# Two broadcasts in a two-layer backbone kernel: through DRAM with a broadcast DMA, in place of matmuls

## The chip, the cores and the metric

The kernel runs on one core of one Trainium2 chip. The metric is the time of one execution on the device in microseconds (us), as the median of several runs. The engines are TensorE (PE; PEld are its weight loads), VectorE (DVE), ScalarE (ACT), GpSimd (POOL) and SyncE (SP), which in this kernel only issues DMAs, one after another from one queue.

## The reference

Two layers, each: a normalisation modulated by c, three token mixers side by side, and one output projection. Cut to what matters here:

```python
def layer_fwd(x, xc, c, c_ctx, ...):                  # x: (1, 256, 1024) latent, xc: (1, 256, 1024) context
    shift, scale, gate = split(silu(c) @ w_mod + b_mod, 3)
    shift_c, scale_c, gate_c = split(silu(c_ctx) @ w_mod + b_mod, 3)
    h  = rms_norm(x, norm_g) * (1 + scale) + shift    # hc for xc in the same way
    p  = [h @ w for w in split_cols(w_in, IN_SIZES)]
    y_a = ssd_branch(...)      # bidirectional scan over chunks of 128 tokens, 16 heads, decays exp(cumsum)
    y_b = diff_branch(...)     # differential attention
    y_c = mlstm_branch(...)    # bidirectional matrix memory over chunks of 128 tokens, 4 heads,
                               # with a running maximum as stabiliser
    mixed = (g[0] * (y_a @ w_branch[0]) + g[1] * (y_b @ w_branch[1]) + g[2] * (y_c @ w_branch[2])) @ w_out
    x_new = x + gate[:, None] * mixed                 # xc_new = xc + gate_c * ...
```

All of it is in float32. The output is x after the second layer.

## The kernel before

The 256 context and 256 latent tokens are four chunks (NT = 4) of P = 128 tokens; group p = 0 is the context, p = 1 the latent tokens. Every float32 operand of a large product is split in a high and a low part (`whi`/`wlo` for weights, `hh`/`hl` for the normalised input, `yh`/`yl` for a branch output), and a product is three matmuls, hi*hi, hi*lo and lo*hi: lines L148 to L150 where tokens stand on the partitions of the result (`mm_tok`), L179 to L181 where channels do (`proj_ch`). Weights come as `raw` tiles of 512 KB (three buffers), ScalarE casts `whi` (L119) and DVE subtracts `wlo` (L82; the helper `tt` puts all its tensor_tensor operations on that line, `stt` on L79).

The order of the instructions on each engine is made by the framework's scheduler from priorities that the source sets with `band(0)`, `band(1)` and `band(2)`: 0 for weight loads, splits and evacuations, 1 for scans and attention, 2 for the projections' matmuls. All DMAs stand in SP's one queue in the order that results.

**The row stage**, once in each layer, makes the per-token numbers of the two scans. The gate rows lie on NR = 64 partitions (two directions of 32) with 512 tokens along the row. At each chunk's end three values for each row are put into `sv` [64, 3, 4] (L613 and lines before it): the end of the cumulated log decay, the running maximum that the chunk starts with, and the one it ends with. Meanwhile r1 and r2 are transposed to tokens on partitions (L626; `ca` and `cb` are the copies, L630). Tokens on partitions also need the twelve end values of each row on every partition: the tile `bcs` [128, 12, 64]. It is made on PE: `sx` is `sv` spread on a diagonal (a product with the identity), and a matmul with ones sums over its 64 partitions, in two halves of 384 columns (L637), each copied from PSUM to `bcs` (L638). From `bcs`, `ca` and `cb` come the columns `col` (SSD) and `mlc` (mLSTM), which scale the operands of the scans. In the same stretch of the program, DVE makes `ux` (SSD inputs after the convolution), which PE transposes (L710), and between these PE runs projections' matmuls.

**The output stage**, once in each layer: the gate `modc[l][:, 16:24, cc]` has channels on partitions (8 columns of 128 channels, cc = 1 for context), and the result has tokens on partitions. So `gbc[p]` [128, 1024] is to hold the gate along the row, the same on every partition. For each of its eight blocks of 128 channels one column of `modc`, repeated 128 times as the stationary operand, is multiplied with the identity (L1247), and ScalarE copies each half from PSUM with a factor 0.5 (L1249). The factor belongs to the merge's sigmoid. `evac_out` multiplies the accumulated output projection by `gbc[p]` (`otmp`) and adds it to the residual (`y`). In layer 0 both groups are worked on, in layer 1 only the latent one, so there are three gbc tiles. The last weight tiles of layer 0's output projection take the buffers `yh`/`yl` (L1297).

Of the kernel before, what the change touches and what calls it, by code (L numbers as in the profile page):

```python
# [14 lines left out]
ALU = mybir.AluOpType  # L15
# [3 lines left out]
D = 1024  # L19
P = 128  # L20
# [9 lines left out]
NR = 64  # L30
# [4 lines left out]
def hybrid_backbone_kernel(ctx: ExitStack, tc: tile.TileContext, A, out, dbg=None):  # L35
    nc = tc.nc
    V, S, G, T = nc.vector, nc.scalar, nc.gpsimd, nc.tensor
# [5 lines left out]
    @contextmanager  # L43
    def band(b):
        saved = tc.cur_priority
        tc.cur_priority = bands[b]
        yield
        bands[b] = tc.cur_priority
        tc.cur_priority = saved

    base = ctx.enter_context(tc.tile_pool(name="base", bufs=1))
    psum = ctx.enter_context(tc.tile_pool(name="psum", bufs=1, space=PSUM))

    def mk(pool, shape, tag, dt=F32, bufs=1):
        if dbg is not None:
            b = 1
            for n in shape[1:]:
                b *= n
            b *= 2 if dt == BF16 else 4
            key = (pool.name, tag)  # L60
            dbg["usage"][key] = max(dbg["usage"].get(key, 0), (b + 31) // 32 * 32 * bufs)
        return pool.tile(list(shape), dt, tag=tag, name=tag, bufs=bufs)

    def pacc():
        return mk(psum, [P, 512], "acc", bufs=ACC)
# [4 lines left out]
    def pm():  # L70
        return mk(psum, [P, 512], "pm", bufs=PM)
# [6 lines left out]
    def stt(o, a, s, b, op0, op1, eng=None):  # L78
        (eng or V).scalar_tensor_tensor(out=o, in0=a, scalar=s, in1=b, op0=op0, op1=op1)  # L79

    def tt(o, a, b, op, eng=None):
        (eng or V).tensor_tensor(out=o, in0=a, in1=b, op=op)  # L82
# [10 lines left out]
    def bc(ap, n):  # L93

        return ap.unsqueeze(len(ap.shape)).to_broadcast(list(ap.shape) + [n])


    ident = mk(base, [P, P], "ident")
# [3 lines left out]
    ones = mk(base, [NR, P], "ones")  # L102
# [6 lines left out]
    modc = [mk(base, [P, 24, 2], "modc", bufs=2) for _ in range(depth)]  # L109
# [340 lines left out]
    for l in range(depth):  # L450
# [84 lines left out]
        rp = tc.alloc_tile_pool(name=f"row{l}", bufs=1)  # L535
# [24 lines left out]
        with band(1):  # L560
# [39 lines left out]
            sv = mk(rp, [NR, 3, NT], "sv")  # L600
            V.memset(sv, 0.0)
            for i in range(NT):
                for d, order in ((0, FWD), (1, BWD)):
                    c = order[i]
# [24 lines left out]
            V.tensor_copy(ca, pa.rearrange("p (c r) -> p c r", r=P))  # L629
            V.tensor_copy(cb_, pb.rearrange("p (c r) -> p c r", r=P))  # L630

            sx = mk(rp, [NR, 12, NR], "sx")
            tt(sx, bc(sv.rearrange("p a c -> p (a c)"), NR), ident[0:NR, 0:NR].unsqueeze(1).to_broadcast([NR, 12, NR]), ALU.mult)
            bcs = mk(rp, [P, 12, NR], "bcs")
            for i in range(2):
                pt = pm()
                T.matmul(pt[:, 0:384], lhsT=ones, rhs=sx[:, 6 * i : 6 * i + 6, :].rearrange("p a r -> p (a r)"), start=True, stop=True)  # L637
                V.tensor_copy(bcs[:, 6 * i : 6 * i + 6, :], pt[:, 0:384].rearrange("p (a r) -> p a r", r=NR))  # L638
            acl, mpb, meb = bcs[:, 0:4, :], bcs[:, 4:8, :], bcs[:, 8:12, :]
            for d in range(2):  # L640
                r_ = slice(32 * d, 32 * d + 16)
# [9 lines left out]
            for d in range(2):  # L651
                r_ = slice(32 * d + 16, 32 * d + 20)
# [66 lines left out]
        chunk = lambda a, c: a[:, c * P : (c + 1) * P]  # L719
# [518 lines left out]
        xnew = Tokens(yx, "y", pq) if not last else xcur  # L1238
        with band(1):
            gbc = {}  # L1240
            for p in pq:
                gbc[p] = mk(ep, [P, D], "gbc", bufs=2)
                cc = 1 - p
                for hf in range(2):
                    pt = pm()
                    for k in range(4):
                        T.matmul(chunk(pt, k), lhsT=modc[l][:, 16 + 4 * hf + k, cc : cc + 1].to_broadcast([P, P]), rhs=ident, start=True, stop=True)  # L1247

                    S.mul(gbc[p][:, hf * 512 : (hf + 1) * 512], pt, 0.5)  # L1249
            if l == 0:  # L1250
                for p in pq:
                    for i in range(2):
                        for g in range(2):
                            src = (A["x"] if p else A["ctx"])[0][i * P : (i + 1) * P, g * 512 : (g + 1) * 512]
                            nc.sync.dma_start(xnew.tile(g, 2 * p + i), src)
# [11 lines left out]
        def evac_out(p, b, ps):  # L1267
            x_ = xnew(b, p)
            tmp = mk(ep, [P, 2, 256], "otmp", bufs=2)
            tt(tmp, ps, gbc[p][:, b * 256 : (b + 1) * 256].unsqueeze(1).to_broadcast([P, 2, 256]), ALU.mult)  # L1270
            tt(x_, x_, tmp, ALU.add)
            if last:
                for i in range(2):
                    nc.sync.dma_start(out[0][i * P : (i + 1) * P, b * 256 : (b + 1) * 256], x_[:, i, :])
# [3 lines left out]
        for b in range(2):  # L1278
            ps = {}
            with band(2):  # L1280
                for p in pq:
                    ps[p] = pacc()
            for k0, hi, lo in granules([wo(b)]):
                with band(2):
                    for p in pq:
                        mm_tok(ps[p], lhs, p * 256 - off, k0, hi, lo)
            for p in pq:
                with band(0):
                    evac_out(p, b, ps[p].rearrange("p (t n) -> p t n", t=2))
# [10 lines left out]
        for p in pq:  # L1300
            for b in (2, 3):
                cs = slice((b - 2) * 256, (b - 1) * 256)
                with band(2):
                    ps = pacc()
                    for g in range(2):
                        mm_tok(ps, lhs, p * 256 - off, 4 * g, wh[:, 4 * g : 4 * g + 4, cs], wl[:, 4 * g : 4 * g + 4, cs])
                with band(0):
                    evac_out(p, b, ps.rearrange("p (t n) -> p t n", t=2))
# [61 lines left out]
```

## Time and profile before

| | |
|---|---|
| median of 3 runs | 1710.55 us (1707.45 to 1711.42) |
| the profiled execution | 1711.2 us, of which the span of the trace is 1709.1 us |
| PE busy | 1677.3 us, 98% of the span |
| DVE busy | 1115.3 us, 65% |
| ACT busy | 762.7 us, 45% |
| POOL busy | 164.0 us, 10% |
| mean granted clock of PE | 0.992 of full speed |

The busy time is that of instructions which the profiler recorded. In rows of the trace, `out<-in` are the program's names of the tiles, a size is partitions x elements, `xN` stands for N instructions, and a bracket at the end of a row says how long the engine stood idle before it and what ended that. The granted clock (PEclk) is a share of the full 2.4 GHz.

### The profile page before, as it was taken

Reading aid. Unit: us, or ns where it says so; the run is one execution under the profiler, and the core shown is the slowest. Engines: PE = TensorE matmul, PEld = TensorE weight load, DVE = VectorE, ACT = ScalarE, POOL = GpSimd, SP = SyncE. Lnnn points to the kernel's source line nnn. Section 1 sums busy time; section 2 is a strip of 40 time slices with the busy share of each in tenths; the row PEclk is TensorE's granted clock in tenths of the full one; section 3 lists DMA queues with packets and bytes.
Section 4 is the critical chain, followed back from the end, with each engine's and each line's share of the span. In section 5 each row is a group of like instructions: output and inputs, shape, how many; then the busy total and the mean of one; then the engine's idle time right before and its main releaser. Section 6 shows DMA issues by size and latency. Waiting matters only on the chain.

```text
span 1709.1 us, 28774 instructions
## 1 busy us (share of the span) xinstructions
PE 1677.3 (98%) x11448; PEld 1489.2 (87%) x11448; DVE 1115.3 (65%) x2183; ACT 762.7 (45%) x1501; POOL 164.0 (10%) x192
## 2 busy tenths in 40 slices
PE   5999999999999999999999999999999999999998
PEld 2787889999899999977777789988999999999998
DVE  4698887667865666623334354898877867765565
ACT  3455644554544444422223233455555555444453
POOL 0102422101100000000010002012121100000100
PEclk8999999999999999999999999999999999999999
DMA  8522122222222222353544442322242324335654
GB/s 262 128 75 62 50 63 65 73 75 63 76 63 75 64 73 64 125 178 96 182 136 131 163 129 51 108 67 75 79 131 71 101 66 130 93 111 173 179 170 146
DMA packets 191906, 180.38 MB, mean 106 GB/s; under 512 B 20606, under 2 KB 177920, under 8 KB 191772
## 3 DMA queue, kind: packets, MB, share of 16 engines
q1 hardware_dynamic: 191772, 178.54, 35.6%
q8 instruction: 90, 1.47, 0.4%
q14 instruction: 44, 0.36, 0.1%
HBM read 177.47 MB, written 1.05 MB: 104 GB/s over the span
## 4 chain that ended last, share of the span: by engine, by line
PE 91%; DVE 4%; DMA 2%; issue 1%; ACT 1%; POOL 0%; SPq 0%; DVEq 0%; ACTq 0%; POOLq 0%
PE acc L149 12%; PE acc L148 12%; PE acc L150 12%; PE acc L179 12%; PE acc L181 12%; PE acc L180 12%; PE pe L917 2%; PE pm L935 2%; DMA wm<-in_w_mod_dram 1%; PE pm L743 1%; PE pm L1088 1%; PE pm L1067 1%; PE pe L228 1%; PE pe L1072 1%; PE pm L775 1%
## 5 line engine op out<-in xcount | busy, mean ns | idle before, releaser
L82 DVE TENSOR_TENSOR wlo<-raw,whi 128x1024 fp32r<-128x1024 f32 x274 | 348.8, 1274 | 308.4 <-ACT whi L119 306.9
L149 PE MATMUL acc<-wlo,hh 128*128 128x256 f32 x1728 | 504.9, 292 | 0.0
L150 PE MATMUL acc<-whi,hl 128*128 128x256 f32 x1728 | 503.1, 291 | 0.0
L148 PE MATMUL acc<-whi,hh 128*128 128x256 f32 x1728 | 501.5, 290 | 0.0
L119 ACT CAST whi<-raw 128x1024 fp32r<-128x1024 f32 x274 | 287.8, 1051 | 383.7 <-PE acc L180 255.0
L149 PEld LDWEIGHTS acc<-wlo,hh 128*128 128x128 f32 x1728 | 330.7, 191 | 12.6 <-issue 9.3
L150 PEld LDWEIGHTS acc<-whi,hl 128*128 128x128 f32 x1728 | 330.8, 191 | 10.4 <-issue 8.4
L148 PEld LDWEIGHTS acc<-whi,hh 128*128 128x128 f32 x1728 | 330.6, 191 | 10.0 <-issue 7.6
L179 PE MATMUL acc<-hh,whi 128*128 128x512 f32 (+1 forms) x712 | 256.3, 363 | 0.0
L180 PE MATMUL acc<-hl,whi 128*128 128x512 f32 (+1 forms) x712 | 254.9, 359 | 0.1
L181 PE MATMUL acc<-hh,wlo 128*128 128x512 f32 (+1 forms) x712 | 253.5, 357 | 0.0
L179 PEld LDWEIGHTS acc<-hh,whi 128*128 128x128 f32 x712 | 134.6, 190 | 27.0 <-issue 6.4
L180 PEld LDWEIGHTS acc<-hl,whi 128*128 128x128 f32 x712 | 135.1, 190 | 19.7 <-issue 3.0
L181 PEld LDWEIGHTS acc<-hh,wlo 128*128 128x128 f32 x712 | 135.1, 190 | 19.5 <-issue 1.9
L179 PE MATMUL acc<-yh,whi 128*128 128x512 f32 (+1 forms) x384 | 128.7, 338 | 0.0
L180 PE MATMUL acc<-yl,whi 128*128 128x512 f32 (+1 forms) x384 | 128.3, 336 | 0.0
L181 PE MATMUL acc<-yh,wlo 128*128 128x512 f32 (+1 forms) x384 | 128.2, 336 | 0.0
L921 ACT ACTIVATE E<-pe,nmax 128x512 f32<-128x512 f32 (+1 forms) x96 | 58.7, 617 | 46.9 <-DVE nmax L919 46.8
L181 PEld LDWEIGHTS acc<-yh,wlo 128*128 128x128 f32 x384 | 71.9, 188 | 8.2
L180 PEld LDWEIGHTS acc<-yl,whi 128*128 128x128 f32 x384 | 72.1, 188 | 8.0
L179 PEld LDWEIGHTS acc<-yh,whi 128*128 128x128 f32 x384 | 72.0, 188 | 7.3
L919 DVE TENSOR_REDUCE nmax<-pe 128x1 f32<-128x512 f32 (+1 forms) x96 | 53.8, 595 | 20.2 <-PE pe L917 19.9
(302 smaller groups left out, 2510.7 us busy)
## 6 DMA issues: line engine op xcount, KB each, us to landing
raw<-in_w_in_dram SPq DMA_DIRECT2D x192, 512.0 KB
raw<-in_w_branch_dram SPq DMA_DIRECT2D x48, 512.0 KB
wm<-in_w_mod_dram SPq DMA_DIRECT2D x45, 512.0 KB
raw<-in_w_in_dram SPq DMA_DIRECT2D x48, 256.0 KB
raw<-in_w_out_dram SPq DMA_DIRECT2D x16, 512.0 KB
raw<-in_w_mod_dram SPq DMA_DIRECT2D x3, 512.0 KB
xin<-in_ctx_dram SPq DMA_DIRECT2D x2, 512.0 KB
xin<-in_x_dram SPq DMA_DIRECT2D x2, 512.0 KB
```

The source lines that it names most:

```text
L82: (eng or V).tensor_tensor(out=o, in0=a, in1=b, op=op)
L119: S.copy(hi, raw)
L148: T.matmul(o, lhsT=xh[:, k, sl], rhs=hi[:, j, :], start=(k == 0 and i == 0), stop=False)
L149: T.matmul(o, lhsT=xh[:, k, sl], rhs=lo[:, j, :], start=False, stop=False)
L150: T.matmul(o, lhsT=xl[:, k, sl], rhs=hi[:, j, :], start=False, stop=(k == KT - 1 and i == 1))
L179: T.matmul(o, lhsT=hi[:, j, cs], rhs=xh[:, k, a:b], start=(k == 0 and first), stop=False)
L180: T.matmul(o, lhsT=hi[:, j, cs], rhs=xl[:, k, a:b], start=False, stop=False)
L181: T.matmul(o, lhsT=lo[:, j, cs], rhs=xh[:, k, a:b], start=False, stop=(k == KT - 1 and final))
L917: T.matmul(es[m][0], lhsT=x[own, qs], rhs=y[own, 0:N], start=(n == 0), stop=(n == 2))
L919: V.tensor_reduce(out=ng[:, m : m + 1], in_=es[m][0], axis=AX.X, op=ALU.max, negate=True)
L921: S.activation(e_, o, AF.Exp, bias=ng[:, m : m + 1], accum_out=rs[:, m : m + 1])
L935: T.matmul(po[:, qs], lhsT=chunk(aT, kt), rhs=vt[:, kt, h * P : (h + 1) * P], start=(kt == 0), stop=(kt == nk - 1))
```

## The change

The values go to DRAM and come back with a DMA that reads the same row for all 128 partitions. In the row stage two DMAs write `sv` (32 rows each, four-byte elements, 384 of them) to a DRAM tile `sv_d` [12, 64], and one DMA broadcasts its 768 values to `bcs` (128 x 3 KB, 393 KB). In the output stage one DMA for each token group writes the gate to `gate_d` (1024 four-byte elements), and one broadcasts it to `gbc` (128 x 4 KB, 512 KB). The factor 0.5 moves into `evac_out`, which takes a scalar_tensor_tensor for the tensor_tensor. `rows_d` is the DRAM pool. All these DMAs are issued by SP, at band 0.

```diff
--- before.py
+++ after.py
@@ -49,6 +49,7 @@
         tc.cur_priority = saved
 
     base = ctx.enter_context(tc.tile_pool(name="base", bufs=1))
+    rows_d = ctx.enter_context(tc.tile_pool(name="rows_d", bufs=1, space=bass.MemoryType.DRAM))
     psum = ctx.enter_context(tc.tile_pool(name="psum", bufs=1, space=PSUM))
 
     def mk(pool, shape, tag, dt=F32, bufs=1):
@@ -629,13 +630,12 @@
             V.tensor_copy(ca, pa.rearrange("p (c r) -> p c r", r=P))
             V.tensor_copy(cb_, pb.rearrange("p (c r) -> p c r", r=P))
 
-            sx = mk(rp, [NR, 12, NR], "sx")
-            tt(sx, bc(sv.rearrange("p a c -> p (a c)"), NR), ident[0:NR, 0:NR].unsqueeze(1).to_broadcast([NR, 12, NR]), ALU.mult)
+            sv_d = mk(rows_d, [12, NR], "sv_d", bufs=2)
             bcs = mk(rp, [P, 12, NR], "bcs")
-            for i in range(2):
-                pt = pm()
-                T.matmul(pt[:, 0:384], lhsT=ones, rhs=sx[:, 6 * i : 6 * i + 6, :].rearrange("p a r -> p (a r)"), start=True, stop=True)
-                V.tensor_copy(bcs[:, 6 * i : 6 * i + 6, :], pt[:, 0:384].rearrange("p (a r) -> p a r", r=NR))
+            with band(0):
+                for r_ in (slice(0, 32), slice(32, NR)):
+                    nc.sync.dma_start(sv_d.rearrange("a r -> r a")[r_, :], sv[r_].rearrange("p a c -> p (a c)"))
+                nc.sync.dma_start(bcs.rearrange("p a r -> p (a r)"), sv_d.rearrange("a r -> (a r)").partition_broadcast(P))
             acl, mpb, meb = bcs[:, 0:4, :], bcs[:, 4:8, :], bcs[:, 8:12, :]
             for d in range(2):
                 r_ = slice(32 * d, 32 * d + 16)
@@ -1238,15 +1238,13 @@
         xnew = Tokens(yx, "y", pq) if not last else xcur
         with band(1):
             gbc = {}
+            gate_d = mk(rows_d, [2, D], "gate_d", bufs=2)
             for p in pq:
                 gbc[p] = mk(ep, [P, D], "gbc", bufs=2)
                 cc = 1 - p
-                for hf in range(2):
-                    pt = pm()
-                    for k in range(4):
-                        T.matmul(chunk(pt, k), lhsT=modc[l][:, 16 + 4 * hf + k, cc : cc + 1].to_broadcast([P, P]), rhs=ident, start=True, stop=True)
-
-                    S.mul(gbc[p][:, hf * 512 : (hf + 1) * 512], pt, 0.5)
+                with band(0):
+                    nc.sync.dma_start(gate_d[cc].rearrange("(k p) -> p k", p=P), modc[l][:, 16:24, cc])
+                    nc.sync.dma_start(gbc[p], gate_d[cc].partition_broadcast(P))
             if l == 0:
                 for p in pq:
                     for i in range(2):
@@ -1267,7 +1265,8 @@
         def evac_out(p, b, ps):
             x_ = xnew(b, p)
             tmp = mk(ep, [P, 2, 256], "otmp", bufs=2)
-            tt(tmp, ps, gbc[p][:, b * 256 : (b + 1) * 256].unsqueeze(1).to_broadcast([P, 2, 256]), ALU.mult)
+
+            stt(tmp, ps, 0.5, gbc[p][:, b * 256 : (b + 1) * 256].unsqueeze(1).to_broadcast([P, 2, 256]), ALU.mult, ALU.mult)
             tt(x_, x_, tmp, ALU.add)
             if last:
                 for i in range(2):
```

What this does to the order of the instructions is shown at three places. On DVE in the row stage of layer 0, before, this is the stretch from the first readers of `bcs` to the third `ux` of that layer (which PE's third group of transposes at L710 reads):

```order
L82 TENSOR_TENSOR col<-bcs,ca 128x4x16
L646 COPY col<-bcs 128x4x16
L82 TENSOR_TENSOR col<-bcs,ca 128x4x16
L646 COPY col<-bcs 128x4x16
L826 TENSOR_REDUCE ssq<-sq 128x8
L82 TENSOR_TENSOR col<-col 128x128
L638 COPY bcs<-pm 128x384
L82 TENSOR_TENSOR mlc<-bcs,cb 128x4x4
L82 TENSOR_TENSOR mlc<-cb,bcs 128x4x4
L79 SCALAR_TENSOR_TENSOR ux<-th,cv_a 128x512
```

Now the stretch from the end of the rows' work (`r_z`) on; lines are shifted by one:

```order
L87 TENSOR_SCALAR r_z_566<-r_z 64x512
L83 TENSOR_TENSOR sm<-r_z_566,sm 64x512
L83 TENSOR_TENSOR wlo<-raw,whi 128x1024
L631 COPY cb<-pm 128x512
L83 TENSOR_TENSOR col<-bcs,ca 128x4x16
L646 COPY col<-bcs 128x4x16
L80 SCALAR_TENSOR_TENSOR ux<-th,cv_a 128x512
L83 TENSOR_TENSOR col<-bcs,ca 128x4x16
L646 COPY col<-bcs 128x4x16
L83 TENSOR_TENSOR mlc<-bcs 128x4x4
```

`sx` and the copies from `pm` are gone, and the first row that needs the broadcast stands right behind `cb`, with the third `ux` behind it. In layer 1 the third `ux` stands ahead of the first such row.

On SP at the same place, before, between the loads of small columns (`gcol`) and weights:

```order
L1167 DMA gcol<-in_ssd_a_log_dram 16x1
L1167 DMA gcol<-in_ml_i_bias_dram 4x1
L130 DMA raw<-in_w_in_dram 128x4x128 x2
L130 DMA raw<-in_w_in_dram 128x4x256 x17
L1167 DMA dbc<-in_ssd_d_dram 128x16
```

and now:

```order
L1167 DMA gcol<-in_ssd_a_log_dram 16x1
L1167 DMA gcol<-in_ml_i_bias_dram 4x1
L131 DMA raw<-in_w_in_dram 128x4x128 x2
L637 DMA sv_d<-sv 32x12x1 x2
L638 DMA bcs<-sv_d 128x768
L131 DMA raw<-in_w_in_dram 128x4x256 x17
L1167 DMA dbc<-in_ssd_d_dram 128x16
```

The two writes and the broadcast stand between the weight loads: the writes wait for `sv`, the broadcast for the writes, and the 17 weight loads behind them for their turn in the queue.

On SP at the end of layer 0, before:

```order
L130 DMA raw<-in_w_out_dram 128x4x256 x2
L1255 DMA y<-in_x_dram 128x512 x2
L130 DMA raw<-in_w_out_dram 128x4x256 x2
L1297 DMA raw<-in_w_out_dram 128x4x256 x3
L1255 DMA y<-in_x_dram 128x512 x2
L1297 DMA raw<-in_w_out_dram 128x4x256
```

and now:

```order
L131 DMA raw<-in_w_out_dram 128x4x256 x2
L1253 DMA y<-in_x_dram 128x512 x2
L131 DMA raw<-in_w_out_dram 128x4x256 x2
L1296 DMA raw<-in_w_out_dram 128x4x256
L1247 DMA gbc<-gate_d 128x1024 x2
L1246 DMA gate_d<-modc 128x8x1
L1296 DMA raw<-in_w_out_dram 128x4x256 x2
L1253 DMA y<-in_x_dram 128x512 x2
L1296 DMA raw<-in_w_out_dram 128x4x256
```

The two broadcasts of layer 0 and the write of layer 1's gate stand behind the first of the `yh` weight loads (L1297 before, L1296 now). The writes of layer 0's gate stand some thirty rows further up, and the broadcast of layer 1 twenty-odd rows further down. On PE the sixteen records at each gate and the L637 rows are gone, and the third group of `ux` transposes in layer 0 has 27 weight matmuls ahead of it since the r2 transposes; the wait ahead of the r2 transposes has the same rows before it.

## Rows read from the trace of the kernel before

**Rows 1.** The page: busy time by engine, and the chain that ended last.

```profile
PE 1677.3 (98%) x11448; PEld 1489.2 (87%) x11448; DVE 1115.3 (65%) x2183; ACT 762.7 (45%) x1501; POOL 164.0 (10%) x192
...
PE 91%; DVE 4%; DMA 2%; issue 1%; ACT 1%; POOL 0%; SPq 0%; DVEq 0%; ACTq 0%; POOLq 0%
```

**Rows 2.** Windows, in order: start:end, length, busy PE PEld DVE ACT POOL, PEclk, DMA, GB/s.

```profile
983.00:1026.00 43.00, 43.00 (x275) 37.31 (x275) 21.97 (x27) 15.81 (x20) 0.00 (x0) 1.00 0.45 127
...
1625.00:1667.00 42.00, 42.00 (x357) 42.00 (x356) 25.58 (x36) 22.36 (x36) 1.44 (x2) 1.00 0.59 172
...
1126.70:1133.70 7.00, 7.00 (x25) 4.97 (x23) 5.42 (x24) 1.35 (x4) 0.00 (x0) 0.51 0.51 150
```

**Rows 3.** Chain that ended last, gate's matmuls: start, us, what.

```profile
922.37 0.89 PE pm L1247 x8
...
1012.23 1.78 PE pm L1247 x16
```

**Rows 4.** The same chain in the two row stages.

```profile
113.36 0.84 PE pm L637 x2
...
115.10 0.12 PE acc L149
...
118.29 0.44 PE pm L710 x4
...
1127.48 1.57 PE pm L637 x2
...
1132.77 1.28 PE pm L637 x2
```

**Rows 5.** PE's timeline, the r2 transposes of both layers, with the wait before.

```profile
112.70 0.66 PE L626 MATMUL pm<-ident,r 128*128 128x128 f32 x4 [1.68 <-ACT r L619]
...
1125.51 0.66 PE L626 MATMUL pm<-ident,r 128*128 128x128 f32 x4 [2.02 <-ACT r L619]
```

**Rows 6.** DVE's timeline, row stage of layer 0.

```profile
111.23 0.32 DVE L613 COPY sv<-r_z 32x1 f32<-32x1 f32 x2
...
114.27 1.23 DVE L82 TENSOR_TENSOR wlo<-raw,whi 128x1024 fp32r<-128x1024 f32 x1 [0.26 <-ACT whi L119]
...
115.41 0.68 DVE L630 COPY cb<-pm 128x512 f32<-128x512 f32 x1
...
118.83 0.69 DVE L79 SCALAR_TENSOR_TENSOR ux<-th,cv_a 128x512 f32<-128x512 f32 x1
```

**Rows 7.** DVE's timeline, row stage of layer 1.

```profile
1124.05 0.31 DVE L613 COPY sv<-r_z 32x1 f32<-32x1 f32 x2
...
1131.02 0.23 DVE L82 TENSOR_TENSOR col<-bcs,ca 128x64 f32<-128x64 f32 x1
```

**Rows 8.** Timelines of SP and DVE: a broadcast load and its reader; the last store.

```profile
712.16 0.34 SPq L1167 DMA_DIRECT2D lamt<-in_diff_lambda_dram  x1
...
715.82 0.29 DVE L82 TENSOR_TENSOR lp<-lamt 128x128 f32<-128x128 f32 x1 [2.43 <-DMA lamt<-in_diff_lambda_dram]
...
1706.14 0.43 SPq L1274 DMA_DIRECT2D out_dram<-y  x1
```

**Rows 9.** Timelines of SP and ScalarE: the narrow columns of w_in (L548), and their cast.

```profile
1020.88 4.63 SPq L548 DMA_DIRECT2D raw<-in_w_in_dram  x6
...
1027.97 2.00 ACT L119 CAST whi<-raw 128x1024 fp32r<-128x1024 f32 x2 [6.38 <-DMA raw<-in_w_in_dram]
```

**Rows 10.** Waits of PE, 86 to 260 us: total us, times, longest.

```profile
PE pm L775 <- DVE M L82: 0.8, 1, 0.8
...
PE pm L743 <- DVE xw L82: 0.5, 1, 0.5
```

**Rows 11.** DVE's groups by line and shape: busy us, mean ns; then idle before.

```profile
L82 DVE TENSOR_TENSOR otmp<-acc,gbc 128x512 f32<-128x512 f32 x12 | 8.2, 683 | 12.8 <-PE acc L150 12.6
```

**Rows 12.** ScalarE's timeline; PE's instructions on yh (x, min/median/max ns, first to last).

```profile
1020.54 1.05 ACT L119 CAST yh<-raw 128x1024 fp32r<-128x1024 f32 x1 [2.20 <-DMA raw<-in_w_out_dram]
...
L148 PE MATMUL acc<-yh,yb x64: 278/281/375, 1032.6 to 1056.6; 128*128 128x256 f32 x64
```

## The prediction

> **What bounds the kernel now.** I read the page first: TensorE (PE) is busy for 1677.3 of 1709.1 us, and the chain that ended last is PE for 91% [rows 1]. So a matmul that is taken out gives its time back, as long as PE has other work ready there and none of what replaces it comes late. I then read the table of windows around each place that the change touches. In the stretches with the gate's matmuls PE has no idle time at all (43.00 of 43.00 us, and 42.00 of 42.00 us), while VectorE (DVE) is busy for 21.97 and 25.58 us of them [rows 2]. The stretch around the gates at 922 us looks the same. So in these stages PE alone sets the pace. The third row of the group is the row stage of layer 1: PE is busy for all of 7.00 us, at a granted clock of 0.51, which is the lower of its two levels (1.2 GHz against 2.4).
>
> The chain gives the price of each removed matmul, since it counts what a group adds to PE's time and not its pipelined length [rows 3, 4]. The timeline of PE shows why the row stage is not full of work: in both layers PE stands for 1.68 and 2.02 us until ScalarE has written r, ahead of the r2 transposes (L626) [rows 5]. The second of these waits is followed by the stretch at 0.51, the first by none. This wait lies ahead of everything that is changed, so I expect it to stay as it is.
>
> **What the change removes.**
> 1. The gate's matmuls (L1247): for each of three token groups eight, which the trace records as sixteen, half of them for each half of gbc. The chain has them as four groups of eight records with 0.89 us each (one stands for the four) and one of sixteen with 1.78 us [rows 3]. 4 x 0.89 + 1.78 = 5.34 us, all in stretches where PE has no gap. What stood behind them is weight products whose operands lay ready, so I count all 5.34 as gained.
> 2. The row stage's matmuls (L637): 0.84 us twice in layer 0 (one stands for both) and 1.57 + 1.28 = 2.85 us in layer 1, at the lower clock [rows 4]. At the full clock the latter are 2 x 0.84 = 1.68 us too. I take 1.68 for layer 1, because the lower clock is not theirs: a stretch at 0.51 that does its work in fewer cycles may end later in the work by as much. 2.85 is the other bound.
> 3. On DVE the building of sx, four copies bcs<-pm, and on ScalarE the six scalings by 0.5. All of it lies off the chain in stages where DVE and ScalarE have idle time. I count nothing for it. The factor 0.5 goes into the evacuation of the output: a SCALAR_TENSOR_TENSOR on 128x512 took 0.69 us [rows 6], the TENSOR_TENSOR that it replaces 683 ns [rows 11]. That is also nothing; if it cost a tenth more, the last evacuation alone would show at the end, by under 0.1 us.
>
> **What it adds.** Two hops through DRAM for each group, all issued by SyncE (SP).
>
> 4. The gates. The writes of layer 0 stand in SP's queue between weight loads of the branch projections, some 30 rows of SP ahead of their gbc, and the write and the gbc of layer 1 are as far apart. So the writes are hidden, and so is the gbc of layer 1, which goes out ahead of that layer's branch projections. At the end of layer 0 two gbc transfers of 512 KB each enter ahead of the w_out loads. In the stretch around it the DMA engines move 127 GB/s at a share of 0.45 [rows 2], so they could move about 127 / 0.45 = 282 GB/s, and 1.05 MB takes them about 3.7 us. The last of the loads behind them is cast at 1020.54 for 1.05 us, and PE reads the first of these weights at 1032.6 [rows 12]. That leaves 1032.6 - 1021.6 - 1.2 (the matching wlo, as in [rows 6]) = 9.8 us, more than 3.7. I count nothing. Without that cover it would be up to 3.7 us.
>
> 5. The end values in layer 0. The last copy to sv ends at 111.55 [rows 6]. SP issues two writes; an issue takes 0.34 to 0.43 us [rows 8], so the second starts at about 111.98. How long a write of four-byte pieces takes to land, no row of before shows. The nearest one is the load of narrow weight columns: six transfers of 1024 small pieces each, the last issued by 1020.88 + 4.63 = 1025.51, and the cast that waits for them starts at 1027.97, so 2.46 us after it [rows 9]. A write of full rows to DRAM has landed 2.96 us after its issue at the latest, since there the span ends (1706.14 to 1709.1) [rows 1, 8]. The longest bound is to count the six as one: 1027.97 - 1020.88 = 7.09 us. I take 2.46 as the nearest in kind. The broadcast back is nearest to that of lamt, issued at 712.16 and read at 715.82, 3.66 us [rows 8]; it is smaller (128 KB against 393 KB), so this is no upper end. So bcs is there at 111.98 + 2.46 + 3.66 = 118.1. Now the order matters: DVE is through with cb at 115.41 + 0.68 = 116.1 [rows 6] and its next row is a col that reads bcs. It stands there for 2.0 us. Behind it stand the third ux and all later work of DVE. Two col rows (0.23 each [rows 7]) and ux (0.69), ends overlapped, bring ux to 119.1. PE leaves the r2 transposes at 112.70 + 0.66 = 113.36, and without L637 it has two groups of four ux transposes (0.44 each) and 27 weight matmuls (0.12 each) ahead of the third group [rows 4, 5]: 113.36 + 0.88 + 3.24 = 117.5. There it waits for 119.1 - 117.5 = 1.6 us. Layer 0 keeps 1.68 - 1.6 = 0.1 us of its gain. Its bounds: no wait at all if the two trips take under 4.6 us together (gain 1.68); the long end is in the rivals.
>
> 6. The end values in layer 1. sv is done at 1124.05 + 0.31 = 1124.36 and before the change the first col that reads bcs started at 1131.02 [rows 7]. By the same trips bcs comes at 1124.36 + 0.4 + 2.46 + 3.66 = 1130.9, just in time. Nothing lost; and ux stands ahead of the wait in this layer.
>
> **The sum.** 5.34 + 1.68 + 0.1 = 7.1 us off the profiled execution's 1711.2 us (span 1709.1 plus 2.1 around it), so 1704.1. The profiled execution lies 0.65 us above the median of 1710.55, so 1703.4 against the median, 0.4% faster. From no change a measurement of this kernel can tell about 0.2%, that is 3.4 us: 1707.1 to 1714.0 counts as the same. The forecast's own range, from no wait and 2.85 us in layer 1 to a wait of 4 us in layer 0, is 1700.5 to 1706.5.
>
> **The rivals.**
> - B, the row stage gives more. Trips of under 4.6 us (gain 1.68), 2.85 us in layer 1, and the rows of the scan, which move ahead in DVE's order, take away PE's waits for M and xw behind it (0.8 + 0.5 us [rows 10]): 5.34 + 1.68 + 2.85 + 1.3 = 11.2. If the stretch at 0.51 (7.00 us, 3.4 of them lost) goes too, 14.6. Middle: 1697.6 against the median. For it speaks that these waits are on DVE rows that the order now has earlier; against it, that the wait that precedes the slow stretch stays.
> - C, a longer wait in layer 0. Both trips at 3.66 us: bcs at 119.3, ux at 120.2, a wait of 2.7 us, after which the clock falls as it did behind the 2.02 us in layer 1 (3.4 us). 1.68 - 2.7 - 3.4 = -4.4, sum 2.6: 1707.9, the same. Against it: PE stood for 1.68 us in layer 0 and the clock stayed.
> - D, slower. The four-byte writes are slow: 7.09 us until they have landed. bcs comes at 122.7 in layer 0, ux at 123.6, PE waits 6.1 us and loses 3.4 to the clock; in layer 1 bcs comes at 1124.8 + 7.09 + 3.66 = 1135.5, 4.5 us behind 1131.02. 5.34 + 1.68 + 1.68 - 6.1 - 3.4 - 4.5 = -5.3: 1715.8. With t for both trips the loss grows by 2 us for each 1 us; at 8.1 us the gain is gone, at 9.8 it is slower by 0.2%. For it: 384 pieces of four bytes in each write is a kind that before has nowhere, and with the queues full of weights they share the engines. Against it: 6144 small pieces took no longer than 7.09 us in all [rows 9].
> - E, the gate's matmuls give nothing back, because PE's next weights come later by as much (the loads set the pace, not PE). Then 1.8 us are left: 1708.8, the same. Against it stand DMA shares of 0.45 and 0.59 beside a full PE [rows 2].
>
> A rule of the Trainium skill speaks for D: the page "DMA: Bandwidth & Descriptors", section "Rules for kernel authors", says that a last dimension which isn't contiguous lowers to one descriptor per element, and that transfers under 64 KB pay mostly overhead. No row of before shows such a write, so the trace neither agrees nor disagrees yet. The same page's section "Anatomy of one DMA — SWDGE (gpsimd) path" puts the fixed part of a DMA at about 2.0 us; by that, as an estimate, the two trips take about 4 us and nothing is waited for in layer 0, which would give 1701.8 instead of 1703.4.
>
> **How the numbers follow.** Forecast 0.50, B 0.18, C 0.14, D 0.11, E 0.07. Faster by over 0.2%: the forecast and B, 0.68. Within it: C and E, 0.21. Slower: D, 0.11. The range runs from B's further half to the upper end of C and E, 1695.5 to 1710; about 0.15 is left out, nearly all of it D.
>
> **What would show it.** Right: no PE gap where the gates were, PE's total busy time lower by about 7 to 8 us, DVE standing about 2 us ahead of its first col in layer 0, with PE waiting some 1.6 us for the third ux. Wrong: an idle PE of over 3 us behind the r2 transposes, a stretch at half clock in layer 0 where there was none, PE waiting for yh weights near 1032 us, or trips through DRAM of over 8 us together.

## The result and the profile after

The changed kernel takes 1725.07 us (median of 4 runs, 1723.41 to 1725.58) against 1710.99 us for the kernel before in the same comparison: a ratio of 1.0083, 95% interval 1.007 to 1.0095. It is 0.8% slower, 14 us, where 0.4% faster was forecast. The profiled execution has a span of 1723.8 us. On its page, the busy times, the DMA packets and the chain that ended last:

```profile
PE 1671.2 (97%) x11392; PEld 1485.4 (86%) x11392; DVE 1108.6 (64%) x2177; ACT 758.6 (44%) x1495; POOL 164.7 (10%) x192
...
DMA packets 197346, 182.75 MB, mean 106 GB/s; under 512 B 25407, under 2 KB 182721, under 8 KB 197213
...
PE 90%; DMA 5%; DVE 3%; issue 1%; ACT 1%; SPq 0%; POOL 0%; DVEq 0%; ACTq 0%
```

PE has 6.1 us less to do than in [rows 1], where 7 to 8 were forecast; the share of DMA in the chain has risen to 5%. So the time is in new waits. PE's waits in the changed kernel, with the total in us, their number and the longest:

```profile
PE pm L710 <- DVE col L83: 8.5, 1, 8.5
...
PE pm L710 <- ACT XT L711: 8.2, 1, 8.2
...
PE acc L149 <- DVE otmp L80: 4.4, 1, 4.4
...
PE pm L627 <- ACT r L620: 3.7, 2, 2.0
```

The last row is that of [rows 5], as expected. The first three are new. In layer 0, PE waits for the third ux behind a col, as forecast, but for 8.5 us and not 1.6. In layer 1, where I had counted no wait, it waits for 8.2 us. And at the end of layer 0, where I had counted nothing either, it waits for 4.4 us. The row stage of layer 0 in the timelines of DVE, SP and PE:

```profile
110.52 0.32 DVE L614 COPY sv<-r_z 32x1 f32<-32x1 f32 x2
...
110.73 0.86 SPq L637 DMA_DIRECT2D sv_d<-sv  x2
...
118.79 0.34 SPq L638 DMA_DIRECT2D bcs<-sv_d  x1
...
124.20 0.23 DVE L83 TENSOR_TENSOR col<-bcs,ca 128x64 f32<-128x64 f32 x1 [8.82 <-DMA bcs<-sv_d]
...
124.45 0.68 DVE L80 SCALAR_TENSOR_TENSOR ux<-th,cv_a 128x512 f32<-128x512 f32 x1
...
125.28 1.09 PE L710 MATMUL pm<-ident,ux 128*128 128x128 f32 x4 [8.54 <-DVE col L83]
```

The last copy to sv is done at 110.84 (0.71 us earlier than in [rows 6]); the second write starts at 111.17. The broadcast that waits for the writes is issued at 118.79, 7.6 us later, and its reader starts 5.4 us after that. DVE stands for 8.82 us, with ux behind it, and PE with it. What the DMA engines moved meanwhile (GB/s in 40 slices from 110.7 to 125 us):

```profile
GB/s 1 0 3 2 4 0 0 0 0 0 0 0 0 0 0 0 0 0 0 0 0 0 0 0 0 0 0 0 0 26 86 129 180 241 235 298 287 375 375 266
```

The write's packets end at about 112.5 (800 under 512 B between 111.5 and 112.5, none from there to 118.8), and the broadcast's first ones come at 121. So the engines were through with the pieces some 6.3 us before the broadcast was issued. The same in layer 1, with ScalarE's timeline:

```profile
1134.41 0.31 DVE L614 COPY sv<-r_z 32x1 f32<-32x1 f32 x2
...
1134.62 0.84 SPq L637 DMA_DIRECT2D sv_d<-sv  x2
...
1139.11 0.68 DVE L80 SCALAR_TENSOR_TENSOR ux<-th,cv_a 128x512 f32<-128x512 f32 x1
...
1145.74 0.34 SPq L638 DMA_DIRECT2D bcs<-sv_d  x1
...
1150.74 0.23 DVE L83 TENSOR_TENSOR col<-bcs,ca 128x64 f32<-128x64 f32 x1 [9.39 <-DMA bcs<-sv_d]
...
1151.23 0.31 ACT L648 ACTIVATE col<-col 128x128 f32<-128x128 f32 x1 [10.46 <-DVE col L83]
...
1152.06 0.57 ACT L711 COPY XT<-pm 128x512 f32<-128x512 f32 x1
...
1152.66 0.66 PE L710 MATMUL pm<-ident,ux 128*128 128x128 f32 x2 [8.17 <-ACT XT L711]
```

Here the second write takes 10.7 us until the broadcast is issued (1135.04 to 1145.74), though the 800 packets of both are through by 1136.3, and the broadcast takes 5.0. The third ux was made in good time at 1139.11, ahead of the wait, as the order showed. But ScalarE stood at `col` (L648), which needs DVE's first reader of bcs, and behind it stood the copy of XT that frees PE's next tile in PSUM: PE waits for that copy. At the end of layer 0, timelines of SP, ScalarE, DVE and PE:

```profile
1013.49 0.82 SPq L1247 DMA_DIRECT2D gbc<-gate_d  x2
...
1014.36 0.43 SPq L1246 DMA_DIRECT2D gate_d<-modc  x1
...
1014.90 2.10 SPq L1296 DMA_DIRECT2D raw<-in_w_out_dram  x2
...
1029.22 1.04 ACT L120 CAST yh<-raw 128x1024 fp32r<-128x1024 f32 x1 [8.83 <-DMA raw<-in_w_out_dram]
...
1030.30 1.23 DVE L83 TENSOR_TENSOR yl<-raw,yh 128x1024 fp32r<-128x1024 f32 x1 [8.65 <-ACT yh L120]
...
1031.44 0.68 DVE L80 SCALAR_TENSOR_TENSOR otmp<-acc,gbc 128x512 f32<-128x512 f32 x1
...
1032.18 0.39 PE L149 MATMUL acc<-whi,yb 128*128 128x256 f32 x1 [4.37 <-DVE otmp L80]
```

The weights for yh are issued at 1014.90 to 1017.00, right behind the write of layer 1's gate, and the cast waits for them until 1029.22, for 8.83 us. DVE stands in front of yl, the evacuation otmp stands behind yl, and PE waits for otmp to give back its accumulator. What the DMA engines do meanwhile and what the clock does after each wait is seen in the windows (columns as in [rows 2]):

```profile
116.00:121.00 5.00, 0.75 (x7) 0.54 (x5) 0.00 (x0) 0.00 (x0) 0.00 (x0) 1.00 0.00 0
...
125.00:130.00 5.00, 4.72 (x22) 4.75 (x23) 3.62 (x18) 4.27 (x17) 1.05 (x1) 0.50 0.01 5
...
1019.00:1026.00 7.00, 7.00 (x62) 7.00 (x61) 1.23 (x1) 1.05 (x1) 0.00 (x0) 1.00 1.32 36
...
1033.00:1036.00 3.00, 3.00 (x16) 3.00 (x16) 2.84 (x5) 1.05 (x1) 0.00 (x0) 0.52 0.55 143
...
1137.00:1144.00 7.00, 7.00 (x58) 6.87 (x57) 4.13 (x17) 2.03 (x4) 0.00 (x0) 1.00 0.55 23
...
1152.00:1158.60 6.60, 5.93 (x21) 4.87 (x22) 6.57 (x11) 6.22 (x18) 3.27 (x3) 0.50 0.00 0
```

From 1019 to 1026 the DMA engines count as fully occupied (a share over 1) but move 36 GB/s, where the stretch in [rows 2] has 127. The gate write's own packets are through by then: over 1000 under 512 B are recorded from 1016 to 1019, and none from 1019 to 1026, where what crawls are the loads issued behind them. In layer 1 the weight load issued behind the two writes crawls too, at 23 GB/s from 1137 to 1144. Behind each of the three waits the granted clock is 0.50 to 0.52, the lower level, for some microseconds: 125 to 130, 1033 to 1036 and 1152 to 1158.6 us.

To see what each place costs, I cut all traces at three instructions of PE: the r2 transposes of both layers and, between them, the first score product of the attention (L917) in layer 0. Each row is one profiled execution.

| PE's time in us | r2 transposes to L917, layer 0 | from there to the r2 transposes of layer 1 | from there to the end |
|---|---|---|---|
| before | 169.2 | 843.6 | 583.6 |
| after | 177.0 | 846.9 | 587.9 |
| forecast for after | 169.1 | 840.0 | 580.1 |
| gate alone | 170.7 | 846.0 | 578.7 |
| row stage alone | 177.7 | 843.7 | 589.1 |
| row stage, 48-byte pieces | 168.1 | 843.6 | 579.9 |
| gate of layer 0 alone | 169.2 | 839.6 | 583.4 |
| row stage, 48-byte pieces, two more hops | 170.8 | 843.9 | 582.8 |
| the best version | 167.6 | 840.2 | 579.5 |

The changed kernel loses at all three places: 7.8, 3.3 and 4.3 us. The last column holds some luck of the clock: in the profile before, the 7.00 us at 0.51 [rows 2] lost about 3.4 us; the gate alone has a clock of 1.00 there, and gains 4.9 us for 1.78 us of matmuls.

### The profile page after: what moved, and what is told of

It reads as the page before. It is cut to its first block, busy times and chain, and to the rows that moved or that the text cites. A ratio compares the mean times of both kernels' runs of the same rounds, so it can differ in the third digit from the quotient of the medians.

```text
span 1723.8 us, 28677 instructions
## 1 busy us (share of the span) xinstructions
PE 1671.2 (97%) x11392; PEld 1485.4 (86%) x11392; DVE 1108.6 (64%) x2177; ACT 758.6 (44%) x1495; POOL 164.7 (10%) x192
## 4 chain that ended last, share of the span: by engine, by line
PE 90%; DMA 5%; DVE 3%; issue 1%; ACT 1%; SPq 0%; POOL 0%; DVEq 0%; ACTq 0%
PE acc L150 12%; PE acc L151 12%; PE acc L149 12%; PE acc L180 12%; PE acc L182 12%; PE acc L181 12%; PE pe L917 2%; PE pm L935 2%; DMA wm<-in_w_mod_dram 2%; PE pm L1088 1%; PE pm L1067 1%; PE pm L743 1%; DMA sv_d<-sv 1%; PE pe L229 1%; PE pe L931 1%; PE pe L1072 1%
```

## The experiments

**The two parts alone.** The first run has the gate's part of the change and the row stage of before, the second the reverse.

> Only the output stage of the change (gate through DRAM, factor 0.5 in the evacuation); the row stage keeps its matmuls. The profile of the changed kernel shows 4.4 us of PE idle at the end of layer 0 behind the late yh weights, and some 1.7 us lost to a lower clock after it. If the three places of the change simply add up, this part gains 5.34 us and loses 6.1: about the time of before, 1710 to 1713 us. Rival (the stall at the end of layer 0 was only there because the row stage had shifted everything): 5.3 us faster, about 1705.5 us.

> Only the row stage of the change (sv through DRAM by four-byte elements); the gate keeps its matmuls. If the parts add up, it carries the whole loss: PE waits of 8.5 and 8.2 us and stretches at the lower clock behind them, less the removed matmuls: 1722 to 1726 us, with DVE waiting some 9 us for bcs in each layer. Rival (the parts lean on each other): clearly less, under 1718 us.

Measured: the gate alone 1709.03 us (ratio 0.9994, 0.9981 to 1.0006), the row stage alone 1724.38 us (1.008, 1.0061 to 1.0098). So the parts nearly add up, and the row stage carries the loss. The gate's part is worth nothing as it stands: the waits of the run with the gate alone, from 1000 to 1040 us, show the stall of the changed kernel again,

```profile
ACT yh L120 <- DMA raw<-in_w_out_dram: 11.6, 2, 8.5
...
PE acc L149 <- DVE otmp L80: 4.0, 1, 4.0
```

and the table has it 2.4 us slower than before there. The rival for this run, that the stall comes from the shifted row stage, falls.

**Pieces or trip, in the row stage.** The same row stage, where only the layout in DRAM differs, so that a row of sv goes out in one piece of 48 bytes:

```diff
-            sv_d = mk(rows_d, [12, NR], "sv_d", bufs=2)
+            sv_d = mk(rows_d, [NR, 12], "sv_d", bufs=2)
...
-                    nc.sync.dma_start(sv_d.rearrange("a r -> r a")[r_, :], sv[r_].rearrange("p a c -> p (a c)"))
+                    nc.sync.dma_start(sv_d[r_, :], sv[r_].rearrange("p a c -> p (a c)"))
...
+            bcs = bcs_.rearrange("p r a -> p a r")
```

> As the run with the row stage alone, with one edit: sv_d lies as [64, 12], so each row goes out as one piece of 48 bytes (64 pieces in place of 768), and bcs is read with a stride. Theory P (the four-byte pieces make the write slow): the time from the write's issue to the broadcast's falls from 8 to 11 us to 2.5 to 4 us, bcs comes at about the time of the forecast, and the kernel is at 1705 to 1711 us. Rival T (a write to DRAM takes this long until it counts as landed, whatever its pieces): 8 to 11 us stay, and so does the time, 1722 to 1726 us.

Measured: 1705.65 us, ratio 0.9974 (0.9961 to 0.9986), below the kernel before. Its timelines of SP and DVE in the two layers:

```profile
111.50 0.80 SPq L637 DMA_DIRECT2D sv_d<-sv  x2
...
113.34 0.34 SPq L638 DMA_DIRECT2D bcs<-sv_d  x1
...
116.98 0.27 DVE L83 TENSOR_TENSOR col<-bcs,ca 128x64 f32<-128x64 f32 x1 [0.81 <-DMA bcs<-sv_d]
...
1123.23 0.80 SPq L637 DMA_DIRECT2D sv_d<-sv  x2
...
1125.41 0.46 SPq L638 DMA_DIRECT2D bcs<-sv_d  x1
...
1130.32 0.27 DVE L83 TENSOR_TENSOR col<-bcs,ca 128x64 f32<-128x64 f32 x1 [0.35 <-DMA bcs<-sv_d]
```

The broadcast is issued 1.84 and 2.18 us after the first write (8.06 and 11.1 with four-byte pieces), and in layer 0 it is read 3.64 us later, close to the 3.66 that I had taken from [rows 8]; in layer 1 it takes 4.91 us. The rival T falls: the same 3 KB through the same DRAM pool, by the same two DMAs, is not slow. The page's packet line shows what differs. Before the change it reads

```profile
DMA packets 191906, 180.38 MB, mean 106 GB/s; under 512 B 20606, under 2 KB 177920, under 8 KB 191772
```

and with pieces of 48 bytes

```profile
DMA packets 192386, 181.17 MB, mean 106 GB/s; under 512 B 20830, under 2 KB 178144, under 8 KB 192252
```

that is 224 more under 512 B, where the changed kernel has 4801 more. The first is the 128 rows of both layers and 16 packets for each of the six added DMAs (128 + 6 x 16 = 224); the second, counted in the same way, the 2 x 768 + 3 x 1024 = 4608 elements and 12 x 16 = 192, within one. So each four-byte element went out as a packet of its own.

**How the cost goes with the number of pieces.** Two more layouts: pieces of 16 bytes (192), and four-byte pieces that land close together, by three writes of 256.

```diff
-            sv_d = mk(rows_d, [12, NR], "sv_d", bufs=2)
+            sv_d = mk(rows_d, [3, NR, NT], "sv_d", bufs=2)          # 16 bytes
...
+                    nc.sync.dma_start(sv_d.rearrange("a r c -> r a c")[r_], sv[r_])
...
+            sv_d = mk(rows_d, [NR, 4, 3], "sv_d", bufs=2)           # four bytes, close together
...
+                for a_ in range(3):
+                    nc.sync.dma_start(sv_d[:, :, a_], sv[:, a_, :])
```

> The row stage alone, with sv_d laid out so that a piece is 16 bytes: 192 pieces for the same 3 KB. The trip from the first write's issue to the broadcast's issue was 8.1 to 11.7 us with 768 pieces of four bytes and 1.8 us with 64 of 48 bytes. Theory N (the cost goes with the number of pieces): 2.5 to 4 us, no long wait, 1705 to 1709 us. Rival S (every piece this small is as slow as four bytes, and 48 bytes lie above some length): 8 us or more, 1720 us or more.

> The row stage alone, again in 768 pieces of four bytes, but each row's twelve land side by side (48 bytes apart from row to row) and not 256 bytes apart; three writes of 256 pieces, of which two (512 pieces) stand behind the last copy to sv. Theory N (the number of pieces counts): 5 to 8 us until the broadcast is issued, 1713 to 1722 us. Rival A (the scattered addresses are what is slow): 2 to 3 us, 1705 to 1709 us.

Measured: 1705.67 us (0.9984, 0.9973 to 0.9995) with 16 bytes, and 1714.87 us (1.0036, 1.0023 to 1.0049) with four bytes close together. SP's timeline of the first,

```profile
111.49 0.82 SPq L637 DMA_DIRECT2D sv_d<-sv  x2
...
113.39 0.34 SPq L638 DMA_DIRECT2D bcs<-sv_d  x1
```

1.90 us from the first write to the broadcast, below the 2.5 to 4 us expected from theory N; and SP and DVE of the second,

```profile
110.25 1.87 SPq L637 DMA_DIRECT2D sv_d<-sv  x2
...
115.31 0.35 SPq L638 DMA_DIRECT2D bcs<-sv_d  x1
...
120.17 0.27 DVE L83 TENSOR_TENSOR col<-bcs,ca 128x64 f32<-128x64 f32 x1 [4.64 <-DMA bcs<-sv_d]
```

5.1 us from the first of these two writes to the broadcast. But part of that is a wait for sv: the last copy ends at 111.59, and the second write starts at 111.61, so only its 256 pieces stand behind that copy, and not 512 as I had expected. From the last write's start to the broadcast's issue, the trips in layer 0 are

| pieces | in the last write | us |
|---|---|---|
| 64 of 48 bytes | 32 | 1.41 |
| 192 of 16 bytes | 96 | 1.46 |
| 768 of four bytes, close together | 256 | 3.70 |
| 768 of four bytes, scattered | 384 | 7.62 |

Rival S falls (16 bytes are not slow). Rival A falls as far as close addresses don't take the cost away: 3.70 us is still 2.2 more than with 16 bytes, and the kernel is slower than before. Whether the distance has a share in it, these runs don't show, since the scattered form also has more pieces behind the last copy. Nor do they separate the number of pieces from their length: four-byte pieces came only in hundreds to a write, and 16-byte pieces only in 96. Four-byte trips also vary: counted from the first write, the 768 pieces took 8.1 and 11.1 us in the two layers of the changed kernel, 9.2 and 11.7 us with the row stage alone; why layer 1 takes longer is open.

**The stall at the end of layer 0.** The gate through DRAM in layer 0 alone, with layer 1's matmuls kept:

```diff
+            if l == 0:
+                ...
+                        nc.sync.dma_start(gate_d[cc].rearrange("(k p) -> p k", p=P), modc[l][:, 16:24, cc])
+                        nc.sync.dma_start(gbc[p], gate_d[cc].partition_broadcast(P))
+            else:
+                ...
+                            T.matmul(chunk(pt, k), lhsT=modc[l][:, 16 + 4 * hf + k, cc : cc + 1].to_broadcast([P, P]), rhs=ident, start=True, stop=True)
```

> The gate through DRAM in layer 0 alone; layer 1 keeps its matmuls, so that no four-byte write stands at the end of layer 0, while the 1 MB of broadcasts still does. Theory P (the write of layer 1's gate in four-byte elements holds the DMA engines for 7 us, and the yh weights stand behind it): no PE wait at the end of layer 0, 3.56 us of matmuls gained, 1706 to 1708 us. Rival G (the 1 MB of broadcasts delays the yh weights): the wait of about 4 us and the lower clock stay, 1711 to 1714 us.

Measured: 1706.18 us, ratio 0.9977 (0.9964 to 0.9989); the middle column of the table gains 4.0 us for 3.56 us of matmuls. The waits from 1000 to 1040 us have no PE row of that place any more, and ScalarE's for the yh weights is

```profile
ACT yh L120 <- DMA raw<-in_w_out_dram: 2.8, 3, 2.0
```

The 1 MB of broadcasts is still there, the write of 1024 four-byte elements isn't: rival G falls. The two writes of layer 0's gate, of the same kind, cost nothing where they stand, between weight loads with time in hand.

**Versions without a four-byte write in a bad place.** Three runs put the parts together.

```diff
+                    T.transpose(pt[0:8, 0:P], modc[l][:, 16:24, cc], ident)
+                    gt = mk(ep, [8, P], "gt", bufs=2)
+                    S.copy(gt, pt[0:8, 0:P])
+                    nc.sync.dma_start(gate_d[cc].rearrange("(k p) -> k p", p=P), gt)
+                    nc.sync.dma_start(gbc[p], gate_d[cc].partition_broadcast(P))
```

The gate is turned like this for all three token groups in the first run, for none in the second, and for layer 1's alone in the third.

> Both parts without four-byte pieces: sv_d in pieces of 48 bytes, and the gate turned on PE first (one transpose of 128x8 for each token group, copied to 8 partitions) and written as 8 pieces of 512 bytes. Theory P: 4.3 us gained in the row stages and 5.34 less about 0.4 for the transposes at the gates, 1700 to 1702 us. Rival G (with the gate written only at the end of layer 0 the broadcasts come later, and the yh weights behind them): a PE wait at the end of layer 0, 1704 to 1708 us.

> sv_d in pieces of 48 bytes, the gate through DRAM in layer 0 alone (its four-byte write lies some 200 us ahead of its use), matmuls for the gate of layer 1. If the gains of the two runs that had one of these each add up (4.3 and 3.8 us): 1701 to 1703 us. Rival (they overlap, because both fill the same wait): 1704 to 1706 us.

> Three edits of the change that no run has shown to cost anything: sv_d in pieces of 48 bytes, layer 0's gate written by four-byte elements some 200 us ahead of its use, layer 1's gate turned on PE and written as rows of 512 bytes, so that no transposes and no four-byte write stand at the end of layer 0. If the parts add up: 1703.7 us (the run with layer 1's gate on matmuls) less 1.78 plus about 0.15 for the transpose, 1701.5 to 1702.5 us. Rival (layer 1's gate stage has its time covered by something else): no better than 1703.7.

Measured: 1702.66 us (0.996, 0.9947 to 0.9973), 1703.71 us (0.9969, 0.9956 to 0.9983) and 1702.32 us (0.9947, 0.9934 to 0.9959). The first two lie 0.7 us above their forecasts, the third inside; it has the lowest median, 8.8 us below the kernel before and 23 below the changed one, which speaks against its rival. The intervals of the three overlap, so their order isn't shown, and the rival isn't settled. In the first there is no PE wait for yh or otmp, so rival G isn't the reason for its 0.7 us. All three have more of PE's waits for xw in the row stages (2.7, 2.0 and 1.7 us); in the first,

```profile
PE pm L744 <- DVE xw L83: 2.7, 2, 1.9
```

where before had 0.5 us in layer 0 [rows 10].

**A late bcs without any four-byte piece.** Pieces of 48 bytes, with two more copies from DRAM to DRAM ahead of the broadcast:

```diff
+                for n_ in range(2):
+                    nxt = mk(rows_d, [NR, 12], f"sv_e{n_}", bufs=2)
+                    nc.sync.dma_start(nxt, sv_d)
+                    sv_d = nxt
```

> The row stage alone with sv_d in pieces of 48 bytes, and two more hops from DRAM to DRAM ahead of the broadcast, so that bcs comes some 4 us later with no four-byte piece anywhere. The scheduler now places both ux of layer 0 ahead of the first row that reads bcs. Theory L (a late bcs costs by itself, since the scans need col): as much as the run with three writes of four-byte pieces, whose bcs came about as late, 1712 to 1716 us. Theory O (it costs by what stands behind the waiting row in DVE's and ScalarE's order, ux and XT above all, while PE has weight products to go on with): little PE waiting in layer 0, 1705 to 1709 us.

Measured: 1713.64 us, ratio 1.0014 (1.0004 to 1.0023), against 0.9974 with the direct trip. SP and DVE in layer 0:

```profile
111.56 0.80 SPq L637 DMA_DIRECT2D sv_d<-sv  x2
...
113.40 0.52 SPq L640 DMA_DIRECT2D sv_e<-sv_d  x1
...
115.42 0.47 SPq L640 DMA_DIRECT2D sv_e<-sv_e  x1
...
117.23 0.35 SPq L642 DMA_DIRECT2D bcs<-sv_e  x1
...
116.14 0.68 DVE L80 SCALAR_TENSOR_TENSOR ux<-th,cv_a 128x512 f32<-128x512 f32 x1
...
121.52 0.27 DVE L83 TENSOR_TENSOR col<-bcs,ca 128x64 f32<-128x64 f32 x1 [3.17 <-DMA bcs<-sv_e]
```

Each hop is 1.8 to 2.0 us here. bcs is read at 121.52, 4.5 us later than at the direct trip, with both ux ahead of it. PE doesn't wait for ux now, but further on:

```profile
PE pm L748 <- DVE xw L83: 4.3, 2, 2.9
...
PE pe L764 <- ACT ex L768: 1.7, 1, 1.7
```

Theory O falls, and L holds in its time: xw and ex need col, and weight products don't fill the gap. The weight loads behind the hops in SP's queue come later too, but in neither row stage does an engine wait for one. So the row stage is paid for by the time until bcs is there, wherever the wait shows; moving ux ahead only moves it.

## Why the prediction was wrong

The mechanism that decided in the row stages was rival D's, to which I gave 0.11, and it was larger than I had it: 1715.8 us forecast for it, 1725.07 measured. The stall at the gate was in none: E has weights that come too late there, but from loads that set the pace, not from a write ahead of them. All four signs of being wrong came, the one at the yh weights by way of otmp.

- **Step 5, the trip in layer 0, failed in the choice of the row.** I took 2.46 us for the write from a load of narrow columns [rows 9]; measured 7.6 us. That row is a load of 1024 pieces, of at least 16 bytes on the side of DRAM, and the write is of single elements. The direction alone, a load taken for a write, isn't it: 16-byte pieces written are fast. With pieces of 48 bytes the step comes near: forecast bcs 6.12 us after the second write's start (111.98 to 118.1), measured 5.05 (111.93 to 116.98), of which the write has 1.41 for 2.46; PE waits 0.7 us for ux, not 1.6, and the layer's stage is 1.1 us shorter, not 0.1. What I had called the longest bound, 7.09 us for all six loads as one, was still below the write's 7.6 and 10.7 us; and the broadcast took 5.4 and 5.0 us, not 3.66, though 4.91 in layer 1 with 48-byte pieces says that this is not the four-byte writes alone.
- **Step 6, layer 1, failed twice:** by the same trip (bcs at 1150.74, 16.0 us after sv was done at 1134.41 + 0.31 = 1134.72), and because I had followed DVE alone. ScalarE's queue has the same kind of wait in front of XT, which PE needs.
- **Step 4, the gates, was right in its matmuls and wrong in "I count nothing".** I had priced the 1 MB of broadcasts (3.7 us, with 9.8 in hand) and left out that a write that nobody waits for still stands ahead of other transfers. The matmuls of layer 0 were worth 4.0 us for 3.56, and 3.4 in the best version; those of layer 1 1.4 us between the last two versions, for 1.78 less a transpose. The order of the last two isn't shown, so that 1.4 is weak. But behind the four-byte write of layer 1's gate the loads of the yh weights crawled for 7 us, and PE stood for 4.37 us.
- **Step 2**, 1.68 us in layer 1, is borne out. With 48-byte pieces the last column gains 3.7 us, but there the stretch at the lower clock is shorter: the granted clock was 0.71, 0.50 and 0.94 in the three windows of 2 us from 1125 to 1131 us, about 1.7 us lost, where before lost about 3.4. That leaves 2.0 us.
- **The clock.** I let a wait of 1.6 us in layer 0 pass without a loss, and with the 0.7 us of the 48-byte pieces it did; behind waits of 8.5, 4.4 and 8.2 us the lower level came each time: half of 125 to 130, 1033 to 1036 and 1152 to 1158.6 us is about 2.5, 1.4 and 3.3 us lost.
- **The range.** Its upper end, 1706.5, is 0.6 above what its terms give (1710.55 less 5.34 + 1.68 + 1.68 - 4 is 1705.9); that decided nothing.

With the measured trips in D's own sum (13.0 and 15.7 us from the second write to the reader): 5.34 + 1.68 + 1.68 - (13.0 - 4.6) - 3.4 - (15.7 - 6.2) = -12.6, that is 1723.1 us, and the 3.3 us that the gates lost rather than gained 3.56 would make it 1730. Both row stages cost less than that sum: 7.8 us in the table for 8.4 + 3.4 - 1.68 = 10.1, and 4.3 for 9.5 - 1.68 - 1.78 = 6.0. The waits and clocks of the traces come nearer. In layer 1 PE waited 8.2 us and lost 3.3 to the clock, less the 3.4 that the profile before lost there, less 1.78 and 1.68 us of matmuls: 4.6 for 4.3. In layer 0 it waited 8.5 us and lost 2.5, less 1.68, less the 1.1 us of waits for xw and ex that before has behind it and the changed kernel hasn't: 8.2 for 7.8. D's sum had missed both clocks of layer 1 and those later waits.

The Trainium skill's rule, in "DMA: Bandwidth & Descriptors", section "Rules for kernel authors", that a last dimension which isn't contiguous lowers to one descriptor per element, holds here: 1632 more packets under 512 B with the row stage alone, which has 1536 elements and six added DMAs (1536 + 6 x 16). I had it down as a rival and priced it by the wrong row. The fixed part of about 2.0 us in the section "Anatomy of one DMA — SWDGE (gpsimd) path", which is a fit for DMAs issued from GpSimd, gave about 4 us for both trips as an estimate; the trace, where SP issues them, has 5.05 with 48-byte pieces, and 13.0 with four-byte ones.

## What to carry to other kernels

A broadcast through DRAM can take matmuls off a full PE, but lay the DRAM tile out so that each partition writes one run of bytes, and let the reader take the stride: for the row stage alone this turned 14 us of loss into a gain of 4 here. Look at how many pieces a DMA has and how short they are, not at its bytes, and at what stands behind it in the queue, even if nothing waits for it. Where a value comes late, follow every engine's order past the row that reads it, not only the engine that makes the next operand.

## What the runs showed of the hardware

Most of the time of a write in four-byte elements comes after its last packet. The DMA engines were through with 768 elements at about 112.5 us and 1136.3 us, but the broadcast that waited for them was issued 6.3 and 9.4 us later; with 64 or 192 longer pieces the packets of layer 0 end within 0.5 us of that issue. In that time loads crawl: the 512 KB load issued at 1136.33 moved at 23 GB/s from 1137 to 1144, and the loads behind 1024 elements of the gate at 36 GB/s from 1019 to 1026, with ScalarE waiting 8.83 us for them. What goes on in that time no trace shows.

The stretch at 0.51 in layer 1 [rows 2] isn't part of every execution: with the gate alone the profiled run had a granted clock of 1.00 from 1129 to 1136 us after the same wait of 2.0 us. Runs of the kernel before with a mean clock of 0.996 took 1705.87 to 1711.25 us, those with 0.991 took 1711.23 to 1713.49; so a difference of some 3 us between single profiles can come from the clock alone.
